# The first stage of a gated encoder layer in one written-out order: values in products of 512 columns, with masks and zero rows loaded in the block stage

## The chip, the core and the metric

The kernel runs on one core of a Trainium2 chip, in one launch. A time is the device time of that launch in microseconds (us); below it is told as the median of several runs. The trace is of one profiled execution.

A core has five engines that run their own instruction streams in order and wait for one another by semaphores: PE (TensorE, matmuls; PEld are its weight loads), DVE (VectorE), ACT (ScalarE), POOL (GpSimd) and SP (SyncE, which here only issues DMAs; its queue is SPq in the trace).

## What is computed

One encoder layer over 1024 tokens of width 1024, all in float32. Cut to what matters here:

```python
h = rmsnorm(x, attn_norm_g)
proj = h @ w_in
(c_q, c_kv, k_rope, z_mla, q_dil, k_dil, v_dil, z_dil, g_mla, g_dil) = jnp.split(proj, ...)
a_out = mla_attention(c_q, c_kv, k_rope, ...)         # 8 heads, latent ranks 256 and 128
d_out = dilated_mixture(q_dil, k_dil, v_dil, ...)     # 3 groups x 8 heads x 64
y_mla = (a_out * silu(z_mla)) @ w_o_mla
y_dil = (d_out * silu(z_dil)) @ w_o_dil
merged = sigmoid(g_mla + b) * y_mla + sigmoid(g_dil + b) * y_dil
out = rmsnorm(x + merged @ w_out, final_norm_g)
```

The change touches the projection: the latents `c_q`, `c_kv`, `k_rope` (416 columns of `w_in`) with the small products behind them, and the dilated values `v_dil` (three groups g of 512 columns each).

## The kernel before

Each float32 operand of a large product is split into a high and a low part, and a product is three matmuls: high by high, high by low, low by high (`mm3`, lines 145 to 147). A split is a copy on ACT (line 151) and a subtraction on POOL or DVE (line 152). The input, transposed and scaled by its norm gain, lies in `hTh` and `hTl` (in the trace `at_r`; in instruction lists `at_8192_r`) from the first microseconds on, in eight chunks `kc` of 128 rows.

The run has three parts. The **first stage** makes the latents, queries, keys and values of the latent attention, the dilated values, and the sums that the block stage needs. The **block stage** (`blocks`) makes dilated queries and keys and some gates in 16 items of seven parts each, a part being 4 x 3 matmuls of 512 columns into banks `st_a` to `st_d`. Then come the attention and the output. The block stage and what follows are issued in a written order (`manual_schedule`). The first stage is issued by the tile scheduler, which chooses the order of the instructions from `run` (lines 1598 to 1637).

In the first stage:

- `latent_proj` makes the 416 latent columns for eight groups t of 128 tokens: 8 x 8 `mm3` calls. ACT squares the results for the norm (lines 262 and 263), DVE copies them to `lat`.
- `token_factors` loads `x` in eight pieces `x_in`, sums their squares on ACT (line 276) and makes the per-token factor `rcol` by a chain of small DVE instructions (`rsqrt`, lines 204 to 210; line 278).
- `tables` makes the sine and cosine tables, stores them to DRAM (`s_cs`) and loads them back in copies `cs_m` and `cs_d`.
- `latents` scales `lat` by the factors (line 358), transposes it on PE (line 365), splits the transposes (lines 368 and 369), and makes queries, keys and values from them. Its 30 results are stored by way of two staging buffers `mla_st`.
- `dil_v(g, quad)` makes the dilated values: for each of three groups and two quads, for each of eight token groups, eight `mm3` calls into 256 columns of a bank `pj`. The result is scaled by `rcol` (lines 446 and 447, or 457) into `dv_st` or `dv_s` and stored.
- `block_sums` loads the input again in 16 pieces `y`, scales them on ACT (line 474), combines four at a time on POOL (lines 476 to 479), and splits the results on ACT and DVE into `s_h` and `s_l`.

PSUM has eight banks. In the first stage six serve the pool of `dil_v` and `latent_proj`, two the pool of `latents` (`NB_A = 6`).

Of the kernel before, what the change touches and what calls it, by code (L numbers as in the profile page):

```python
# [10 lines left out]
F32 = mybir.dt.float32  # L11
# [8 lines left out]
S = 1024  # L20
# [19 lines left out]
NB_A = 6  # L40
# [21 lines left out]
class Net:  # L62
# [170 lines left out]
    def latent_proj(self, lp, wl, xp, pj):  # L233
# [9 lines left out]
        for half in range(2):  # L243
            ps = [pj.tile([128, 512], F32, name="pj") for _ in range(4)]
            todo = []
            for kc in range(8):
                self.load_x(half, kc, xp)
                if half == 0:
                    raw = wl.tile([128, 416], F32, name="wl_raw", bufs=3)
                    self.dma(raw, a["wl"][kc])  # L250
                    self.split(raw, h[:, kc], l[:, kc], nc.gpsimd if kc % 2 else v)
                for t in range(4):
                    todo.append((kc, t))
            if half:
                todo.sort(key=lambda x: x[1])
            for kc, t in todo:
                ts = slice(512 * half + 128 * t, 512 * half + 128 * t + 128)
                self.mm3(ps[t][:, :416], self.hTh[:, kc, ts], self.hTl[:, kc, ts], h[:, kc], l[:, kc], kc == 0, kc == 7)
            for t in range(4):
                i = 4 * half + t  # L260
                junk = xp.tile([128, 256], F32, name="x_junk", bufs=2)
                nc.scalar.activation(out=junk, in_=ps[t][:, 0:256], func=AF.Square, accum_out=self.lss[:, 0, i:i + 1])
                nc.scalar.activation(out=junk[:, 0:128], in_=ps[t][:, 256:384], func=AF.Square, accum_out=self.lss[:, 1, i:i + 1])
                v.tensor_copy(self.lat[:, i, 0:400], ps[t][:, 0:400])
                v.tensor_copy(self.lat[:, i, 416:432], ps[t][:, 400:416])
            if half == 0:
                v.tensor_scalar(out=self.hb, in0=self.hb, scalar1=0.5, scalar2=None, op0=ALU.mult)

    def token_factors(self, xp, pp):

        nc, a = self.nc, self.a
        ss = xp.tile([128, 8], F32, name="x_ss", bufs=1)
        for t in range(8):
            x = xp.tile([128, D], F32, name="x_in")
            self.dma(x, a["x"][128 * t:128 * t + 128, :])
            nc.scalar.activation(out=x, in_=x, func=AF.Square, accum_out=ss[:, t:t + 1])
        y = self.rsqrt(ss, 1.0 / D, xp, 8)
        nc.vector.tensor_copy(self.rcol, y)
        pt = pp.tile([128, 512], F32, name="pj")
        nc.tensor.transpose(pt[:8, :128], y, self.ident)  # L280
        row = xp.tile([8, 128], F32, name="x_row", bufs=1)
        nc.vector.tensor_copy(row, pt[:8, :128])
        self.dma(self.rs, row)
        flat = self.rs.rearrange("a b -> (a b)")
        self.dma(self.R, flat.partition_broadcast(128))

    def tables(self, tp):
# [4 lines left out]
        self.dma(pi, a["positions"].partition_broadcast(64))  # L292
        ang = tp.tile([64, S], F32, name="ang", bufs=1)
# [21 lines left out]
    def rope(self, pa, pb, cos, sin, tp):  # L315
# [3 lines left out]
        m = [tp.tile([128, 512], F32, name=f"rope_m{i}") for i in range(4)]  # L319
# [6 lines left out]
    def up_weights(self, lp):  # L326
# [5 lines left out]
        for i in range(3):  # L332
            raw = lp.tile([128, 1024], F32, name="u_raw")
            n = 768 if i < 2 else 1024
            self.dma(raw[:, :n], a["wuq"][:, 768 * i:768 * i + 768] if i < 2 else a["wukv"])
            self.split(raw[:, :n], uh[:, i] if i < 2 else kh, ul[:, i] if i < 2 else kl, nc.gpsimd)
        return uh, ul, kh, kl

    def latents(self, up, lp, tp, pj):

        nc, a = self.nc, self.a
        v = nc.vector
        uh, ul, kh, kl = up
        for half in range(2):
            c512 = slice(half * 512, half * 512 + 512)

            r = self.rcol[:, 4 * half:4 * half + 4]
            sc = tp.tile([128, 2, 4], F32, name="lat_sc")
            for i in range(2):
                v.scalar_tensor_tensor(out=sc[:, i], in0=self.lss[:, i, 4 * half:4 * half + 4], scalar=(0.5, 1.0)[i], in1=r, op0=ALU.mult, op1=ALU.mult)  # L350
                v.tensor_tensor(out=sc[:, i], in0=sc[:, i], in1=r, op=ALU.mult)
            y = self.rsqrt(sc.rearrange("p a b -> p (a b)"), 1.0 / 128, tp, 8)
            for i in range(2):
                v.tensor_tensor(out=y[:, 4 * i:4 * i + 4], in0=y[:, 4 * i:4 * i + 4], in1=r, op=ALU.mult)
            for t in range(4):
# [294 lines left out]
    def blocks(self, items, tp, pp):  # L650
# [6 lines left out]
        for n in range(2):  # L657
            self.block_loads(n, items[n])
# [1082 lines left out]
```

## Time and profile before

| | |
|---|---|
| median of 3 runs | 1227.03 us (1226.45 to 1229.11) |
| the profiled execution's own time | 1229.1 us |
| its span, first to last instruction | 1227.1 us |
| PE busy | 1204.8 us, 98% of the span |
| DVE, ACT, POOL busy | 59%, 50%, 47% of the span |
| first matmul of the block stage | at 224.80 us |

The span is 2.0 us shorter than the execution's own time, and this execution is the slowest of the three runs: 2.1 us over their median. Times in the trace are counted from the span's start. A matmul's duration in the trace reaches beyond the start of the next one, since they are pipelined; what a matmul costs in a row of matmuls is the distance between starts.

### The profile page before, as it was taken

To read this page: it belongs to the slowest core of one execution; us is meant where nothing else is said; L and a number is where in the kernel's file an instruction comes from. 1 tells how busy PE (TensorE), PEld (TensorE's weight loads), DVE (VectorE), ACT (ScalarE), POOL (GpSimd) and SP (SyncE) were. 2 spreads that over 40 slices of the span, in tenths; PEclk is the share of its full clock that TensorE was granted. 3 is DMA by queue.
4 is the path that set the end of the run, shared out by engine and by line. 5 is a ranking of instruction groups with operands and counts; after the bars stand their busy time and mean duration, and the time that the engine had idled before them with its cause. 6 is when DMAs were issued, how large, how long until landed. Compare 5 with 4: busy or idle time off the path is not lost.

```text
span 1227.1 us, 19477 instructions
## 1 busy us (share of the span) xinstructions
PE 1204.8 (98%) x6909; PEld 1061.2 (86%) x6909; DVE 729.4 (59%) x1304; ACT 611.9 (50%) x1284; POOL 579.1 (47%) x490
## 2 busy tenths in 40 slices
PE   8989999999999999999999999999999999999997
PEld 7989999888888888888989898888888888888886
DVE  7483534376566753346666666647667767769442
ACT  6533335443434434446564756546556555654222
POOL 1361218777777777643365633416730101158322
PEclk9989999999999999999999999999999999999999
DMA  9858579356536544286889897965473445235241
GB/s 336 233 160 306 192 288 335 104 146 165 158 106 182 152 132 129 103 239 216 242 231 285 222 296 214 277 181 124 155 194 95 119 104 140 78 112 177 81 154 52
DMA packets 126416, 221.37 MB, mean 180 GB/s; under 512 B 28072, under 2 KB 60400, under 8 KB 121392
## 3 DMA queue, kind: packets, MB, share of 16 engines
q1 hardware_dynamic: 126320, 220.14, 60.4%
q8 instruction: 54, 0.88, 0.3%
q14 instruction: 42, 0.34, 0.1%
HBM read 149.24 MB, written 70.85 MB: 179 GB/s over the span
## 4 chain that ended last, share of the span: by engine, by line
PE 78%; DMA 9%; DVE 3%; ACT 3%; POOL 3%; issue 2%; SPq 1%; ACTq 0%; POOLq 0%; DVEq 0%
PE bank L145 6%; PE bank L147 6%; PE bank L146 6%; PE bank L871 4%; PE st_a L145 2%; PE st_a L147 2%; PE st_a L146 2%; PE st_c L146 2%; PE st_d L146 2%; PE st_d L145 2%; PE st_c L145 2%; PE st_d L147 2%; PE st_c L147 2%; PE bank L896 2%; PE bank L895 2%
## 5 line engine op out<-in xcount | busy, mean ns | idle before, releaser
L152 POOL TENSOR_TENSOR w_l<-w_raw,w_h 128x512 fp32r<-128x512 f32 x188 | 245.8, 1321 | 234.6 <-ACT w_h L151 183.2
L151 ACT CAST w_h<-w_raw 128x512 fp32r<-128x512 f32 x188 | 112.2, 620 | 106.3 <-POOL w_raw L496 90.6
L145 PE MATMUL bank<-at_r,w_h 128*128 128x512 f32 x344 | 141.3, 411 | 0.0
L146 PE MATMUL bank<-at_r,w_h 128*128 128x512 f32 x344 | 134.8, 392 | 0.6 <-POOL at_r L152 0.6
L147 PE MATMUL bank<-at_r,w_l 128*128 128x512 f32 x344 | 135.0, 392 | 0.0
L879 DVE TENSOR_TENSOR at_r<-bank,at_r 128x512 fp32r<-128x512 f32 x128 | 87.8, 687 | 68.0 <-ACT at_r L873 67.5
L873 ACT CAST at_r<-bank 128x512 fp32r<-128x512 f32 x128 | 74.9, 585 | 82.0 <-PE bank L871 81.2
L147 PE MATMUL pj<-w_h,at_r 128*128 128x256 f32 x384 | 109.7, 286 | 0.0
L146 PE MATMUL pj<-w_l,at_r 128*128 128x256 f32 x384 | 109.6, 286 | 0.0
L145 PE MATMUL pj<-w_h,at_r 128*128 128x256 f32 x384 | 109.6, 285 | 0.0
L496 POOL TENSOR_TENSOR w_raw<-w_raw 128x512 f32<-128x512 f32 x64 | 82.9, 1295 | 0.1
L871 PE MATMUL bank<-consts,at_f 128*128 128x128 f32 x512 | 76.8, 272 | 0.5 <-DVE at_r L879 0.5
L147 PEld LDWEIGHTS bank<-at_r,w_l 128*128 128x128 f32 x344 | 64.5, 188 | 14.5
L147 PEld LDWEIGHTS pj<-w_h,at_r 128*128 128x128 f32 x384 | 74.3, 194 | 1.0
L146 PEld LDWEIGHTS pj<-w_l,at_r 128*128 128x128 f32 x384 | 74.3, 193 | 0.8
L145 PEld LDWEIGHTS pj<-w_h,at_r 128*128 128x128 f32 x384 | 74.3, 193 | 0.7
L1144 DVE TENSOR_TENSOR at_r<-bank,at_r 128x512 fp32r<-128x512 f32 x64 | 43.9, 685 | 51.5 <-ACT at_r L1140 51.2
L146 PEld LDWEIGHTS bank<-at_r,w_h 128*128 128x128 f32 x344 | 65.0, 189 | 9.7 <-POOL at_r L152 1.0
L145 PEld LDWEIGHTS bank<-at_r,w_h 128*128 128x128 f32 x344 | 64.9, 189 | 8.8
L896 PE MATMUL bank<-at_r,at_r 128*128 128x256 f32 x256 | 66.9, 283 | 1.4 <-DVE at_r L879 1.4
L895 PE MATMUL bank<-at_r,at_r 128*128 128x256 f32 x256 | 66.9, 282 | 0.0
L1125 ACT ACTIVATE at_f<-at_f,at_f 128x256 f32<-128x256 f32 x128 | 64.1, 504 | 3.8 <-DVE at_f L1118 3.7
(325 smaller groups left out, 3328.2 us busy)
## 6 DMA issues: line engine op xcount, KB each, us to landing
w_raw<-wt SPq DMA_DIRECT2D x48, 512.0 KB, 3.7
at_r<-s_dq SPq DMA_DIRECT2D x32, 512.0 KB, 8.1
s_dk<-dq_st SPq DMA_DIRECT2D x80, 128.0 KB, 2.3
s_dv<-dv_st SPq DMA_DIRECT2D x32, 256.0 KB, 3.4
s_dq<-dq_st SPq DMA_DIRECT2D x64, 128.0 KB, 2.4
zt<-s_gt SPq DMA_DIRECT2D x32, 256.0 KB, 3.5
w_raw<-wv SPq DMA_DIRECT2D x12, 512.0 KB, 5.7
at_r<-s_dk SPq DMA_DIRECT2D x8, 576.0 KB, 10.3
```

What stands on the lines that cost most here:

```text
L145: mm(out, lh, rh, start=start, stop=False, skip_group_check=skip)
L146: mm(out, lh, rl, start=False, stop=False, skip_group_check=skip)
L147: return mm(out, ll, rh, start=False, stop=stop, skip_group_check=skip)
L151: self.nc.scalar.copy(out=h, in_=raw)
L152: sub.tensor_tensor(out=l, in0=raw, in1=h.bitcast(F32), op=ALU.subtract)
L496: self.nc.gpsimd.tensor_tensor(out=b[out], in0=b[x], in1=b[y], op=ALU.subtract)
L871: self.nc.tensor.transpose(pt[:, o:o + 128], self.P[k, b][:, 128 * kc:128 * kc + 128], self.ident)
L873: self.nc.scalar.copy(out=h, in_=pt)
L879: self.nc.vector.tensor_tensor(out=l, in0=pt, in1=h.bitcast(F32), op=ALU.subtract)
L895: mm(out, vv[:, kc], ph[:, x], start=kc == 0, stop=False)
L896: mm(out, vv[:, kc], pl[:, x], start=False, stop=kc == 7)
L1125: nc.scalar.activation(out=p, in_=p, func=AF.Exp, scale=-1.0, bias=nm, accum_out=den)
```

## The change

The scheduler no longer orders the first stage. `manual_schedule` now covers the whole run, and a new function `first_stage` writes the order out.

- **Values of 512 columns.** `dil_v` gives way to `v_load`, `v_split` and `v_part`. The two quads of a group lie side by side in one weight tile of 512 columns. The work is cut into 48 parts c: 16 for each group g, each for one token group t and one half s of the chunks kc, 4 `mm3` calls of 512 columns. Two parts fill a bank, and the second of them scales and stores it. Four banks serve the values, four the latents.
- **Latents between the parts.** `latents` becomes a generator of 36 steps. From part 6 on, 1.75 steps follow each part. The up weights are split on DVE instead of POOL, and `mla_st` has five buffers, which the raw up weights use first.
- **First products.** The latent products are ordered by hand (`first_products`); the loads of `x` and the tables are placed between them.
- **Block sums in steps.** `block_sums` becomes a generator; one step follows each part from part 30 on, with `y` in three buffers.
- **Block operands.** The first item's weights are loaded at part 35, and its first five operands are split in parts 44 to 47, with the subtraction on DVE. `w_h` and `w_l` of the blocks alternate between the two pools in fours instead of singly.
- **Moved into the block stage.** Masks, zero rows of `s_dk` and `s_dv`, the zero fill of `s_dq2` and the products of `cs_d` with the token factors (`self.R`) now stand at parts 2 to 24 of the block stage.

The core of the diff:

```diff
-NB_A = 6
+LATENTS_BEGIN, LATENTS_PACE = 6, 1.75
...
+    def v_split(self, s, i, eng):
+
+        wp = (self.wp, self.wpx)[s]
+        h = wp.tile([128, 512], F32R, name="w_h", bufs=4)
+        l = wp.tile([128, 512], F32R, name="w_l", bufs=4)
+        self.split(self.v_raw[s][i // 2][:, i % 2].rearrange("p q c -> p (q c)"), h, l, eng)
+        self.v_w[s, i] = h, l
+
+    def v_part(self, c, pool, tp):
+
+        g, r = divmod(c, 16)
+        part, t = divmod(r, 4)
+        t += 4 * (part // 2)
+        s = (0, 1, 1, 0)[part] ^ (g & 1)
+        begin = part % 2 == 0
+        if begin:
+            self.v_ps[t] = pool.tile([128, 512], F32, name="pj")
+        ps = self.v_ps[t]
+        sl = slice(128 * t, 128 * t + 128)
+        for i in range(4):
+            kc = 4 * s + i
+            self.mm3(ps, self.hTh[:, kc, sl], self.hTl[:, kc, sl], *self.v_w[s, i], begin and i == 0, not begin and i == 3)
+        if begin:
+            return
...
     def block_sums(self, sp, tp):
...
+        for kc in range(3):
+            loads(kc)
+        yield
+        yield
+        scaled(0)
+        yield
+        for kc in range(4):
+            added(kc)
+            if kc:
+                parts(kc - 1)
+                if kc == 1:
+                    loads(3)
+                yield
+            yield
+            if kc < 3:
+                scaled(kc + 1)
+                yield
+        yield
+        parts(3)
...
+            for c in range(48):
+                self.v_part(c, pj, vp)
+                g, r = divmod(c, 16)
+                if 2 <= c < 10:
+                    self.latent_scaled(c - 2)
+                if 5 <= c < 8:
+                    next(weights)
+                if c == 20:
+                    self.token_row(tp, pl)
+                first, second = (0, 1) if g & 1 else (1, 0)
+                if r == 6:
+                    self.v_load(g + 1, first)
+                if r == 14:
+                    self.v_load(g + 1, second)
+                if g < 2 and 12 <= r < 15:
+                    for i in ((0, 1), (2,), (3,))[r - 12]:
+                        self.v_split(first, i, nc.gpsimd if g == 0 else nc.vector)
+                if g and r < 3:
+                    for i in ((0, 1), (2,), (3,))[r]:
+                        self.v_split(1 - (g & 1), i, nc.gpsimd if g == 1 else nc.vector)
+                if c == 29:
+                    self.cos_d, self.sin_d = self.table(dpool, "cs_d", 0)
+                if c == 35:
+                    self.block_loads(0, self.block_items[0], (self.wp, None))
+                if c >= LATENTS_BEGIN and latents:
+                    steps += LATENTS_PACE
+                    while steps >= 1 and latents:
...
+                elif later and c >= 30:
+                    next(later, None)
+                if c >= 44:
+                    for j in ((0, 1), (2,), (3,), (4,))[c - 44]:
+                        self.block_minus(j, self.block_items)
+                        self.block_operand(j, self.block_items, nc.vector)
...
+            if x in (2, 3, 4, 5):
+                y, c = (self.cos_d, self.sin_d)[x // 2 - 1], slice(512 * (x % 2), 512 * (x % 2) + 512)
+                self.nc.gpsimd.tensor_tensor(out=y[:, c], in0=y[:, c], in1=self.R[:, c], op=ALU.mult)
...
+            if x in (4, 8, 12, 16):
+                i = x // 4 - 1
+                self.dma(self.dq[2][i].rearrange("e c r h (a b) f m -> (e c r) (h a) (b f m)", a=2), self.zero.unsqueeze(1).to_broadcast([128, 4, 512]))
...
+            ctx.enter_context(tc.manual_schedule())
```

How the instructions move is read from the order in which each engine gets them. On PE, where the first transposes of the latents stand among the value products, before (`w_h`, `w_l`: value weights; `lat`: the latents; `pj`: a bank):

```order
L145 MATMUL pj<-w_h,at_8192_r 128x256
L365 MATMUL pj<-consts,lat 128x128 x2
L146 MATMUL pj<-w_l,at_8192_r 128x256
L147 MATMUL pj<-w_h,at_8192_r 128x256
L145 MATMUL pj<-w_h,at_8192_r 128x256
L365 MATMUL pj<-consts,lat 128x128 x2
```

The same place now, at the end of part 6 (the transposes are line 421 of the changed file):

```order
L145 MATMUL pj<-w_h,at_8192_r 128x512
L146 MATMUL pj<-w_l,at_8192_r 128x512
L147 MATMUL pj<-w_h,at_8192_r 128x512
L421 MATMUL pj<-consts,lat 128x128 x4
L145 MATMUL pj<-w_h,at_8192_r 128x512
```

The value matmuls are twice as wide, and the transposes of a step stand together after a whole part. From the first matmul of the block stage on, PE's list is the same as before.

On SP, where the pieces `y` of the block sums are loaded, before (`s_mv`, `s_dv_69`: results to DRAM; `wt`: weights of the first block item):

```order
L141 DMA s_mv<-mla_st 128x1024
L141 DMA s_dv_69<-dv_st 32x4x512
L141 DMA w_raw<-wt 128x1024
L141 DMA y_1534<-xt 128x512
L141 DMA y_1537<-xt 128x512
```

The same loads now, from part 28 on (`wv`: value weights of group 2):

```order
L141 DMA s_dv_69<-dv_st 32x4x1024 x2
L141 DMA cs_d<-s_cs 32x2048 x4
L141 DMA s_dv_69<-dv_st 32x4x1024
L141 DMA w_raw<-wv 128x2x256 x4
L141 DMA y_1570<-xt 128x512
L141 DMA y_1572<-xt 128x512
```

The four loads of `cs_d`, which stood far ahead of the `y` loads, now stand just before the last value weights and these. Each DMA uses one of eight semaphores in turn, and its issue waits until the DMA that used that one before it has landed, so that the first `y` load waits for the first `cs_d` load.

On ACT, from the last scaled bank of group 1 (part 31) on, now (line 552: the scaling of `y`; line 151: the high part of a split):

```order
L522 ACTIVATE dv_st<-pj,rcol 128x8x64
L151 CAST w_h<-w_raw 128x512 x2
L552 ACTIVATE y_1570<-y_1570,consts 128x512
L552 ACTIVATE y_1572<-y_1572,consts 128x512
L552 ACTIVATE y_1574<-y_1574,consts 128x512
L552 ACTIVATE y_1576<-y_1576,consts 128x512
L151 CAST w_h<-w_raw 128x512 x2
```

Before, the first four scalings stood between scaled banks of the values, with no value weight behind them:

```order
L474 ACTIVATE y_1540<-y_1540,consts 128x512
L474 ACTIVATE y_1543<-y_1543,consts 128x512
L457 ACTIVATE dv_s_2236<-pj,rcol 128x256
L474 ACTIVATE y_1558<-y_1558,consts 128x512
L474 ACTIVATE y_1561<-y_1561,consts 128x512
L151 CAST s_h<-y_1543 128x512
```

Now the last two of the four value weights that parts 36 to 39 need are copied behind the scaling of four `y` pieces.

More of the change, by code (lines that the diff above doesn't have):

```diff
@@ new lines, in first_products @@
+        for kc in range(8):
+            self.load_x(0, kc, xp)
+            raw = wl.tile([128, 416], F32, name="wl_raw", bufs=3)
+            self.dma(raw, a["wl"][kc])
+            self.split(raw, h[:, kc], l[:, kc], nc.gpsimd if kc % 2 else v)
+            for t in range(4):
+                product(t, kc)
+            if kc == 5:
+                next(tables)
+        for kc in range(8):
+            self.load_x(1, kc, xp)
+        for t in range(4, 8):
+            for kc in range(8):
+                product(t, kc)
@@ new lines, in first_products, with load, squares @@
+        ss = xp.tile([128, 8], F32, name="x_ss", bufs=1)
+        xs = {}
+        def load(t):
+            xs[t] = xp.tile([128, D], F32, name="x_in")
+            self.dma(xs[t], a["x"][128 * t:128 * t + 128, :])
+        def squares(t):
+            nc.scalar.activation(out=xs[t], in_=xs[t], func=AF.Square, accum_out=ss[:, t:t + 1])
+        self.v_load(0, 0)
+        for t in range(3):
+            load(t)
+        next(tables)
+        for t in range(4):
+            squared(t)
+            taken(t)
@@ new lines, in first_products @@
+        for i in range(4):
+            self.v_split(0, i, nc.gpsimd)
+        for t in range(3):
+            squares(t)
+            if t < 2:
+                load(t + 3)
+        next(tables)
+        squared(4)
+        taken(4)
+        self.v_load(0, 1)
+        for t in range(5, 8):
+            squares(t - 2)
+            load(t)
+            if t == 5:
+                next(tables)
+            if t == 6:
+                for i in range(4):
+                    self.v_split(1, i, nc.gpsimd)
+            squared(t)
+            taken(t)
@@ L277, in token_factors, with token_row @@
+        for t in range(6, 8):
+            squares(t)
+        run_all(tables)
         y = self.rsqrt(ss, 1.0 / D, xp, 8)
-        nc.vector.tensor_copy(self.rcol, y)
+        v.tensor_copy(self.rcol, y)
+        v.tensor_scalar(out=self.hb, in0=self.hb, scalar1=0.5, scalar2=None, op0=ALU.mult)
+    def token_row(self, tp, pp):
+        nc = self.nc
         pt = pp.tile([128, 512], F32, name="pj")
-        nc.tensor.transpose(pt[:8, :128], y, self.ident)
-        row = xp.tile([8, 128], F32, name="x_row", bufs=1)
+        nc.tensor.transpose(pt[:8, :128], self.rcol, self.ident)
+        row = tp.tile([8, 128], F32, name="mla_st", bufs=5)
@@ L345, in latents @@
             c512 = slice(half * 512, half * 512 + 512)
[L347 to L355, printed above, removed]
[L356 to L358 removed]
+            cos, sin = self.cos_m[:, c512], self.sin_m[:, c512]
             nh = lp.tile([128, 3, 512], F32R, name="lat_h", bufs=1)
@@ L483, in block_loads, with scaled @@
-    def block_loads(self, n, item):
-        raw = [self.raw_pools[n % 2].tile([128, 8, 128], F32, name="w_raw", bufs=2) for _ in range(2)]
+                    x = y[kc, i, k] = tp.tile([128, 512], F32, name=f"y{i}{k}", bufs=3)
+                    self.dma(x, a["xt"][i, :, kc + 4 * k])
+        def scaled(kc):
+            for i in range(2):
+                for k in range(2):
+                    c = kc + 4 * k
+                    nc.scalar.mul(y[kc, i, k], y[kc, i, k], self.ga[:, c:c + 1])
@@ L486, in block_loads @@
+    def block_loads(self, n, item, pools):
+        raw = [pools[n % 2].tile([128, 8, 128], F32, name="w_raw", bufs=2) for _ in range(2)]
         for i in range(2):
@@ L650, in blocks @@
     def blocks(self, items, tp, pp):
[L652 to L654 removed]
+        pools = self.wp, tp
         places = 7 * len(items)
         steps, ps = {}, {}
[L657 to L660 removed]
@@ L1637, in run @@
+                self.block_items = [(T_QK + (g * 2 + quad) * 4 + which * 2, g, quad, which) for quad in range(2) for g in range(3) for which in range(2)] + [(T_ZM + i,) for i in BLOCK_GATES]
+                cp.tile([128, 896], F32, name="masks")
+                self.masks = self.hand(2048, 896)
+                self.first_stage(cp, dpool, sums)
                 self.rings()
```

357 lines of the change are left out of this document (175 added, 182 removed).

## Prediction

> **What bounds the kernel now.** First the page's head and the waits of PE over the first stage.
>
> ```profile
> PE 1204.8 (98%) x6909; PEld 1061.2 (86%) x6909; DVE 729.4 (59%) x1304; ACT 611.9 (50%) x1284; POOL 579.1 (47%) x490
> ```
>
> ```profile
> PE pj L145 <- ACT wl_h L151: 5.8, 1, 5.8
> PE pj L365 <- DVE lat_l L369: 3.4, 1, 3.4
> PE st_a L145 <- ACT dv_s L457: 2.0, 1, 2.0
> PE pj L365 <- DVE lat L358: 1.2, 1, 1.2
> PE pj L145 <- DVE mla_st L152: 0.4, 1, 0.4
> ```
>
> PE works nearly all the time, so a change pays in two ways: less time for PE's own work, or fewer waits. These five waits are 12.8 us, of which 5.8 come before the first matmul. The others fall mostly at the first latent transposes (1.2 and 3.4) and at the first block matmul (2.0), which waits for ACT to empty a value bank. The timeline of PE has the end of the stage:
>
> ```profile
> 224.80 0.50 PE L145 MATMUL st_a<-at_r,w_h 128*128 128x512 f32 x1 [2.02 <-ACT dv_s L457]
> ```
>
> From here on PE's list is the same in both kernels, so I forecast by how much this moment comes earlier. Next, the stretches behind the two longest waits (length; busy time of PE, PEld, DVE, ACT, POOL; granted clock; DMA):
>
> ```profile
> 74.00:78.00 4.00, 4.00 (x19) 3.87 (x20) 2.52 (x5) 0.24 (x1) 3.85 (x4) 0.50 0.92 276
> 78.00:82.00 4.00, 4.00 (x30) 4.00 (x29) 3.21 (x5) 2.53 (x5) 3.33 (x2) 0.82 0.57 189
> 226.00:228.00 2.00, 2.00 (x7) 1.58 (x6) 0.00 (x0) 0.15 (x1) 2.00 (x2) 0.55 0.28 82
> 228.00:230.00 2.00, 2.00 (x7) 1.55 (x7) 0.00 (x0) 0.81 (x2) 0.37 (x1) 0.60 0.79 260
> ```
>
> A wait costs more than itself. Behind the 3.4 us one the clock was 0.50 and then 0.82: 4 x 0.50 + 4 x 0.18 = 2.7 us of PE's time lost. Behind the 2.0 us one it was 0.55 and 0.60: 2 x 0.45 + 2 x 0.40 = 1.7 us.
>
> **The change part by part.** *Values of 512 columns.* Starts of matmuls in PE's timeline, in the last value product, in the block stage, and in a latent product between narrower ones, and one of three like groups:
>
> ```profile
> 220.22 0.28 PE L146 MATMUL pj<-w_l,at_r 128*128 128x256 f32 x1
> ...
> 222.50 0.28 PE L147 MATMUL pj<-w_h,at_r 128*128 128x256 f32 x1
> ```
>
> ```profile
> 300.00 0.39 PE L145 MATMUL st_d<-at_r,w_h 128*128 128x512 f32 x1
> ...
> 305.67 0.39 PE L146 MATMUL st_b<-at_r,w_h 128*128 128x512 f32 x1
> ```
>
> ```profile
> 163.51 0.40 PE L145 MATMUL pj<-lat_h,ukv_h 128*128 128x512 f32 x1
> 163.74 0.40 PE L146 MATMUL pj<-lat_l,ukv_h 128*128 128x512 f32 x1
> ```
>
> ```profile
> L145 PE MATMUL pj<-w_h,at_r 128*128 128x256 f32 x384 | 109.6, 285 | 0.0
> ```
>
> The first pair is 19 steps apart: 2.28 / 19 = 0.120 us for 256 columns. The second is 25 apart: 5.67 / 25 = 0.2268 us for 512. Before, 3 x 384 = 1152 matmuls take 138.2 us; now 576 take 130.6 us: **7.6 us saved**. At the 0.23 of the third pair it would be 132.5 us and 5.7 saved. I take the first, since a part has twelve wide matmuls in a row, as in the block stage.
>
> [...]
>
> *The old waits.* The 1.2, 3.4 and 2.0 us go if nothing takes their place: 6.6 us, and 2.7 + 1.7 = 4.4 us of clock with them. At the block start, the latents' four banks are long empty, and the scaled value banks belong to the second block item. That makes 7.6 + 6.6 + 4.4 = **18.6 us** at most. What is late next?
>
> *First transposes.* They now stand behind part 6 and need four tokens' groups scaled by DVE.
>
> ```profile
> 10.09 1.42 PE L145 MATMUL pj<-wl_h,at_r 128*128 128x416 f32 x4
> 11.35 0.35 PE L146 MATMUL pj<-wl_l,at_r 128*128 128x416 f32 x1
> ...
> 13.62 0.35 PE L146 MATMUL pj<-wl_l,at_r 128*128 128x416 f32 x1
> ```
>
> ```profile
> 52.62 0.17 DVE L210 SCALAR_TENSOR_TENSOR rs_y<-rs_u,rs_y 128x8 f32<-128x8 f32 x1
> 52.81 0.17 DVE L278 COPY rcol<-rs_y 128x8 f32<-128x8 f32 x1
> ```
>
> ```profile
> L358 DVE TENSOR_SCALAR lat<-lat,rs_y 128x128 f32<-128x128 f32 x8 | 6.7, 832 | 0.0
> L358 DVE TENSOR_SCALAR lat<-lat,rs_y 128x256 f32<-128x256 f32 x8 | 2.8, 346 | 0.0
> L152 DVE TENSOR_TENSOR mla_st<-pj,mla_st 128x512 fp32r<-128x512 f32 x16 | 11.1, 692 | 23.1 <-ACT mla_st L151 23.1
> L151 ACT CAST mla_st<-pj 128x512 fp32r<-128x512 f32 x16 | 9.4, 586 | 22.5 <-DMA s_kn<-mla_st 9.1 <-PE pj L147 5.4 <-DMA s_qn<-mla_st 3.4
> ```
>
> PE: sixteen latent matmuls have started before 11.35 (a chunk is twelve, and four more stand in the first row), and twelve start from 11.35 to 13.62, so 0.189 us each; 176 more end at 44.6. Seven parts of 12 x 0.2268 = 2.72 us bring PE to 63.7. DVE: `rcol` at 53.0 as before, 18 small instructions 0.19 apart (3.4), four groups at 0.35 + 0.83 + at most 0.35 (6.1), and two banks emptied in between at 0.69: 63.9. So the two arrive together. I take 0.5 us of wait. The bounds are 0, and 3.5 with 2.7 of clock if `rcol` comes 3 us later, since the last loads of `x` now stand behind squares that ACT takes in order.
>
> *Weights behind `y`.* This is the new wait that I trust least. The last value weights (needed from part 36 on) are copied by ACT behind four scalings of `y`, and the first `y` load is issued only when the first `cs_d` load, issued behind part 29, has landed (SP's list).
>
> ```profile
> w_raw<-wv SPq DMA_DIRECT2D x12, 512.0 KB, 5.7
> ...
> y<-xt SPq DMA_DIRECT2D x16, 256.0 KB, 5.5
> ...
> cs_d<-s_cs SPq DMA_DIRECT2D x4, 256.0 KB, 10.1
> ```
>
> ```profile
> L151 ACT CAST w_h<-w_raw 128x512 fp32r<-128x512 f32 x30 | 17.7, 621 | 6.2 <-POOL w_raw L496 3.7 <-DMA w_raw<-wv 1.7 <-PE pj L147 0.7
> ...
> L474 ACT ACTIVATE y<-y,consts 128x512 f32<-128x512 f32 x16 | 11.1, 718 | 2.0 <-DMA y<-xt 1.9
> ```
>
> ```profile
> L152 DVE TENSOR_TENSOR s_l<-y,s_h 128x512 fp32r<-128x512 f32 x16 | 19.2, 1230 | 29.0 <-ACT s_h L151 28.5
> ```
>
> From the `cs_d` issue: 10.1 to land, 5.5 for `y`, 4 x 0.72 = 2.9 to scale, 0.6 to copy the third weight, 1.2 on DVE: 20.3 us. PE gets there after six and a half parts less the 0.59 + 0.69 that part 29's bank takes before the issue: 17.7 - 1.3 = 16.4. That is a wait of 3.9 us. If `cs_d` lands in the 5.5 us of `y`, which is as large, it is 15.7 us and no wait. Before, `cs_d` had many other loads in flight, now fewer, so I take the middle, 2.0 us, and 1.0 for the clock (a wait of 2.0 cost 1.7 once, one of 1.2 nothing in the rows). [...]
>
> *The rest* I put at 1.0 us, a little over twice the small wait of 0.4 in the first list. The order gives ACT, DVE and SP the same number of latent results as before, with five staging buffers where there were two.
>
> *Block stage.* Four products of `cs_d` move to POOL's parts 2 to 5, and 13 DMAs to SP's parts 4 to 24.
>
> ```profile
> 224.80:523.30 298.50, 298.50 (x1310) 246.99 (x1311) 165.89 (x265) 124.31 (x236) 216.13 (x171) 0.99 0.49 139
> ```
>
> ```profile
> L1632 POOL TENSOR_TENSOR cs_d<-cs_d,at_f 128x512 f32<-128x512 f32 x4 | 6.2, 1569 | 19.3 <-DMA s_dv<-dv_st 19.3
> ```
>
> POOL is busy 72% there. In four parts, 10.9 us, it has 7.9 + 6.2 = 14.1 us to do and falls 3.2 us behind, while operands are split five parts (13.6 us) ahead. DMA is at 0.49. I cost this at nothing; without that lead it would be 3.2 us.
>
> *Sum.* 18.6 - 0.5 - 2.0 - 1.0 - 1.0 = 14.1 us. The profiled execution would go from 1229.1 to 1215.0; against the median of 1227.0 that is **1213 us** (1212.9).
>
> **The rivals.**
>
> *The first transposes still wait* (chance 0.09). If `rcol` comes 3 us later, DVE is late by 3.5 us and the clock costs 2.7: 18.6 - 3.5 - 2.7 - 4.0 = 8.4, thus 1218.6 us. For it: the two arrive within 0.2 us of each other by the sum. Against it: the order puts nothing else on DVE there.
>
> *Width pays only by columns* (0.04). If a wide matmul costs two narrow ones, 0.240, the first term is gone and the time is 1212.9 + 7.6 = 1220.5. For it: the 0.23 in a mixed stretch. Against it: 25 steps at 0.2268 with the same operands in their other roles. [...]
>
> *ACT and POOL take turns* (0.09), and the kernel is slower. In parts 30 to 47 ACT empties value banks in its order behind copies that wait for POOL's sums.
>
> ```profile
> L476 POOL TENSOR_TENSOR y<-y,y 128x512 f32<-128x512 f32 x4 | 5.2, 1298 | 6.0 <-ACT y L474 6.0
> L477 POOL TENSOR_TENSOR y<-y,y 128x512 f32<-128x512 f32 x4 | 5.9, 1487 | 0.2
> L478 POOL TENSOR_TENSOR y<-y,y 128x512 f32<-128x512 f32 x4 | 6.2, 1560 | 0.3
> L479 POOL TENSOR_TENSOR y<-y,y 128x512 f32<-128x512 f32 x4 | 6.3, 1563 | 1.6 <-ACT y L474 1.4
> L151 ACT CAST s_h<-y 128x512 fp32r<-128x512 f32 x16 | 9.8, 617 | 8.7 <-POOL y L476 2.7 <-POOL y L478 2.6 <-POOL y L479 1.9
> ```
>
> A round is 2.9 of scaling, 5.9 of sums and 2.5 of copies. Strung on one another they make 11.3 us, against three parts of 2.72 = 8.2: 3.1 us late in each of four rounds, 12.4 in all, with 3.9 at part 36 and the clock at 1.7 for each of four waits: 23.1 us, thus 1227.0 - 18.6 + 23.1 = 1231.5 us. Against it: the scaling of the next round stands ahead of the copies, so that POOL can go on meanwhile, and 5.9 fits in 8.2. It decides when `y` lands so late that POOL finds nothing scaled.
>
> *The change moves no time* (0.03): the stage would be held by loads, not PE. Against it stand 98% and PE's unbroken rows.
>
> **How the numbers follow.** My forecast has 0.75. Its bounds are all new waits gone (18.6, thus 1208.4) and the wider pitch with 3.9 + 1.7 at part 36 and the rest (16.7 - 7.1 = 9.6, thus 1217.4). The range of 1206 to 1222 us takes these, 2 us below for waits that also vanish elsewhere, and the first two rivals: 0.88 of the cases, some 0.8 with what the durations leave open. About 0.2% (2.5 us) is what a measurement of this kernel can tell from no change. Faster by more: 0.75 + 0.09 + 0.04 = 0.88; within it 0.03; slower 0.09.
>
> **What would show it.** In the profile of the changed kernel: the first block matmul at about 212 us instead of 224.80 (the 14.1 less the 1.7 of clock that fall behind it); 576 value matmuls 0.227 us apart; no wait of 3.4 us at the transposes; a wait of about 2 us on DVE's `w_l` at part 36; the clock at 1.0 behind the block start; and no new wait from there on. The forecast is wrong if the first block matmul comes before 207 or after 218 us, or if PE waits in the block stage.

## The result, and the profile after

| | before | after |
|---|---|---|
| median of the first comparison, 6 runs each | 1228.36 us (1226.45 to 1229.26) | 1219.16 us (1216.37 to 1222.17) |
| after over before | | 0.9924, 95% interval 0.9907 to 0.9941 |
| the profiled execution's own time | 1229.1 us | 1216.4 us |
| its span | 1227.1 us | 1214.6 us |
| first matmul of the block stage | 224.80 us | 208.49 us |

One execution of the experiments, in `moved_back`, took 1488.66 us at a granted clock of 0.753 and is left out of the times there. The changed kernel is faster: 9.2 us by the medians, 12.5 by the two spans. The spans flatter it, since the profiled execution is the fastest of six after and the second slowest of six before. In a second comparison (the experiment `again`) it took 1216.85 against 1229.51 us, 12.7 us less, ratio 0.99 (0.9878 to 0.9921). The forecast was 14.1 less.

The page's first line, and all waits of PE in the run:

```profile
PE 1193.9 (98%) x6333; PEld 1027.4 (85%) x6333; DVE 740.5 (61%) x1286; ACT 606.7 (50%) x1260; POOL 558.3 (46%) x474
```

```profile
PE pj L145 <- ACT wl_h L151: 6.1, 1, 6.1
PE bank L1069 <- DVE at_r L1052: 4.1, 3, 2.5
PE pj L146 <- DVE w_l L152: 1.6, 2, 0.9
PE bank L1305 <- ACT at_f L1298: 0.9, 3, 0.6
PE bank L146 <- POOL at_r L152: 0.5, 1, 0.5
PE bank L1044 <- DVE at_r L1052: 0.5, 1, 0.5
PE right L1281 <- DMA at_r<-s_dk: 0.2, 1, 0.2
```

All waits of the old first stage are gone but the one ahead of the first matmul. One new one stands there, at part 36. In PE's timeline, with the first transposes and one product of the block stage's last item:

```profile
63.43 0.60 PE L421 MATMUL pj<-consts,lat 128*128 128x128 f32 x4
...
176.28 0.50 PE L146 MATMUL pj<-w_l,at_r 128*128 128x512 f32 x1 [0.90 <-DVE w_l L152]
...
177.98 0.50 PE L146 MATMUL pj<-w_l,at_r 128*128 128x512 f32 x1 [0.74 <-DVE w_l L152]
...
184.01 0.39 PE L145 MATMUL pj<-w_h,at_r 128*128 128x512 f32 x1
...
208.26 0.39 PE L147 MATMUL pj<-w_h,at_r 128*128 128x512 f32 x1
208.49 0.39 PE L145 MATMUL st_a<-at_r,w_h 128*128 128x512 f32 x1
...
496.13 0.39 PE L145 MATMUL st_a<-at_r,w_h 128*128 128x512 f32 x1
```

The same product before:

```profile
514.20 0.39 PE L145 MATMUL st_a<-at_r,w_h 128*128 128x512 f32 x1
```

From 184.01 to 208.26 are 107 steps, 0.2266 us each. The transposes wait for nothing. The block stage starts 224.80 - 208.49 = 16.3 us earlier, and its last item 514.20 - 496.13 = 18.1 earlier, since no clock is lost at its start. In between PE never waits (stretches as in the prediction):

```profile
224.00:512.00 288.00, 288.00 (x1273) 238.46 (x1272) 165.98 (x266) 119.21 (x227) 209.57 (x173) 1.00 0.52 149
```

So far 18.1 us are won, but the span is only 12.5 shorter: **5.6 us are lost again** in the attention, where the two kernels have the same instructions. PE's waits there (line 1069: values of the latent attention), and what DVE waits for just ahead of them:

```profile
847.10 0.38 PE L1069 MATMUL bank<-at_r,at_r 128*128 128x256 f32 x1 [1.41 <-DVE at_r L1052]
...
889.27 0.39 PE L1069 MATMUL bank<-at_r,at_r 128*128 128x256 f32 x1 [2.45 <-DVE at_r L1052]
```

```profile
845.76 0.69 DVE L1617 TENSOR_TENSOR at_f<-at_f,at_f 128x512 f32<-128x512 f32 x1 [4.60 <-DMA at_f<-s_rr]
...
887.92 0.69 DVE L984 SCALAR_TENSOR_TENSOR at_f<-zt,bank 128x512 f32<-128x512 f32 x1 [5.60 <-DMA zt<-s_gt]
```

The same DVE instructions before (with a wait of PE of 1.17 us behind the second and none behind the first):

```profile
861.32 0.69 DVE L1444 TENSOR_TENSOR at_f<-at_f,at_f 128x512 f32<-128x512 f32 x1 [3.21 <-DMA at_f<-s_rr]
...
902.23 0.69 DVE L811 SCALAR_TENSOR_TENSOR at_f<-zt,bank 128x512 f32<-128x512 f32 x1 [4.34 <-DMA zt<-s_gt]
```

DVE names DMA as what it waited for; PE's row names only DVE, which stands between. Both loads (shares of the softmax, `s_rr`, and the first gate, `s_gt`) come 1.3 to 1.4 us later than before, measured by DVE's wait. Behind the longer wait the clock falls as well:

```profile
890.00:892.00 2.00, 2.00 (x9) 1.61 (x7) 2.00 (x3) 1.62 (x3) 0.00 (x0) 0.56 0.82 218
892.00:894.00 2.00, 2.00 (x12) 1.80 (x10) 0.77 (x2) 1.77 (x4) 0.10 (x1) 0.58 0.71 277
```

That is 2 x 0.44 + 2 x 0.42 = 1.7 us. Together 1.41 + (2.45 - 1.17) + 1.7 = 4.4 of the 5.6; the rest lies in small waits: the lead over the kernel before falls from 18.2 us at 526 us of the changed kernel's trace to 17.1 at 763.

### The profile page after: what moved, and what is told of

Its sections match the earlier page's. It is cut to its first block, busy times and chain, and to the rows that moved or that the text cites. A ratio compares the mean times of both kernels' runs of the same rounds, so it can differ in the third digit from the quotient of the medians.

```text
span 1214.6 us, 18187 instructions
## 1 busy us (share of the span) xinstructions
PE 1193.9 (98%) x6333; PEld 1027.4 (85%) x6333; DVE 740.5 (61%) x1286; ACT 606.7 (50%) x1260; POOL 558.3 (46%) x474
## 4 chain that ended last, share of the span: by engine, by line
PE 82%; DMA 10%; POOL 2%; DVE 2%; ACT 1%; issue 1%; SPq 1%; POOLq 0%; ACTq 0%; DVEq 0%
PE bank L146 6%; PE bank L147 6%; PE bank L145 5%; PE pj L146 5%; PE pj L147 5%; PE pj L145 5%; PE bank L1044 4%; PE st_d L145 2%; PE st_c L145 2%; PE st_a L145 2%; PE st_a L146 2%; PE st_c L146 2%; PE st_d L146 2%; PE st_d L147 2%; PE st_c L147 2%; PE st_a L147 2%
## 5 line engine op out<-in xcount | busy, mean ns | idle before, releaser
L152 POOL TENSOR_TENSOR w_l<-w_raw,w_h 128x512 fp32r<-128x512 f32 x175 | 230.2, 1328 | 214.8 <-ACT w_h L151 163.9
L1046 ACT CAST at_r<-bank 128x512 fp32r<-128x512 f32 x128 | 74.9, 585 | 84.9 <-PE bank L1044 84.3
L146 PE MATMUL pj<-w_l,at_r 128*128 128x512 f32 x192 | 75.0, 391 | 1.6 <-DVE w_l L152 1.6
L145 PE MATMUL pj<-w_h,at_r 128*128 128x512 f32 x192 | 75.3, 392 | 0.0
L147 PE MATMUL pj<-w_h,at_r 128*128 128x512 f32 x192 | 74.8, 390 | 0.0
L1313 ACT CAST at_r<-bank 128x512 fp32r<-128x512 f32 x64 | 37.5, 586 | 53.3 <-PE bank L1305 52.2
L1044 PEld LDWEIGHTS bank<-consts,at_f 128*128 128x128 f32 x512 | 59.3, 140 | 1.3 <-DVE at_r L1052 0.9
L1069 PEld LDWEIGHTS bank<-at_r,at_r 128*128 128x128 f32 x256 | 48.7, 190 | 10.1 <-DVE at_r L1052 4.9
```

The costliest lines, as they stand in the source:

```text
L145: mm(out, lh, rh, start=start, stop=False, skip_group_check=skip)
L146: mm(out, lh, rl, start=False, stop=False, skip_group_check=skip)
L147: return mm(out, ll, rh, start=False, stop=stop, skip_group_check=skip)
L152: sub.tensor_tensor(out=l, in0=raw, in1=h.bitcast(F32), op=ALU.subtract)
L1044: self.nc.tensor.transpose(pt[:, o:o + 128], self.P[k, b][:, 128 * kc:128 * kc + 128], self.ident)
L1046: self.nc.scalar.copy(out=h, in_=pt)
```

## The experiments

Each is compared with the kernel before on the same chip. Medians are of 5 to 12 runs. The first four ran together; with them the changed kernel itself stands at 0.99 (`again`; 0.9924 in the first comparison). `pool_sum`, `gates_first`, `all_three` and `before_again` ran on another chip, where the changed kernel was not measured; they are set against 0.99 by their ratio to the kernel before. A ratio's interval reaches about 0.002 (2 to 3 us) to either side, so smaller differences between two edits are not told apart by the times.

**again.** No edit.

> The changed kernel once more, unaltered. In its first profile the first block matmul starts 16.3 us earlier than before (208.49 against 224.80), the last item of the block stage 18.1 us earlier, but the span is only 12.5 us shorter: 5.6 us are given back in the attention, 1.41 us at 847.1 and 2.45 us (with 1.7 of clock behind it) at 889.3, where DVE waits for a load of s_rr and for one of s_gt. Theory A (the loss belongs to the new timing): both waits come again, 1 to 3 us each, and the time is 9 to 13 us under the kernel before. Theory B (the loss is the chance of one execution, since the instructions and their order are the same in both kernels there): one wait or both are gone or of another length, by over 1 us, while the first block matmul stays within 1 us of 208.5.

The first block matmul came at 209.19 us. PE waited 2.09 us at 847.50 and 2.42 at 889.65. Theory A: the loss belongs to the kernel. (Part 36 cost 0.61 + 0.89 + 0.73 here.)

**narrow.**

```diff
-            self.mm3(ps, ..., *self.v_w[s, i], ...)
+            for q in range(2):
+                x = slice(256 * q, 256 * q + 256)
+                self.mm3(ps[:, x], ..., *(y[:, x] for y in self.v_w[s, i]), ...)
```

> Every value matmul of 512 columns is issued as two of 256, in the same order and with the same operands. By the starts in the trace before (0.120 us for 256 columns, 0.2268 for 512) 1152 x 0.120 - 576 x 0.2268 = 7.6 us are lost: first block matmul at about 216.1 instead of 208.5, time 7.6 us above the changed kernel's. Rival 1 (a matmul costs its columns only): no loss, 208.5. [...]

Its first block matmul:

```profile
215.53 0.40 PE L145 MATMUL st_a<-at_r,w_h 128*128 128x512 f32 x1
```

That is 7.0 us later than in the changed kernel, and 7.4 with the waits at part 36 taken off both (1.3 here, 1.6 there). The time was 1223.56 us, 6.7 above `again` (ratio 0.9955, 0.9938 to 0.9971). The rival falls; the width pays what the starts said.

**cs_early.**

```diff
-                if c == 29:
+                if c == 24:
                     self.cos_d, self.sin_d = self.table(dpool, "cs_d", 0)
```

> The four loads of cs_d are issued behind part 24 instead of part 29. Theory (they are what holds the last value weights and the y loads behind them up): PE's waits of 0.90 and 0.74 us at part 36 go, the first block matmul comes at about 206.9, 1.6 us earlier, and the time is 1.6 us under the changed kernel's. Rival (the weights' own load, or ACT's order with the scaling of y ahead of them, sets the wait): the waits stay within 0.5 us.

```profile
177.54 0.50 PE L146 MATMUL pj<-w_l,at_r 128*128 128x512 f32 x1 [0.73 <-DVE w_l L152]
...
208.05 0.39 PE L145 MATMUL st_a<-at_r,w_h 128*128 128x512 f32 x1
```

One of the two waits went, the other stayed on the same split by DVE: by the two profiles `cs_d` is the cause of 0.9 of the 1.6 us. The block stage comes 0.4 us earlier than in the changed kernel's first profile and 1.1 earlier than in `again`, not at the expected 206.9. 1215.71 us, 1.1 under `again`, with overlapping intervals (0.9868 to 0.9903): the times alone don't show a gain.

**moved_back.** The bodies go, unaltered, from `blocks` to `first_stage` (the conditions alone are shown):

```diff
-            if x in (2, 3, 4, 5):
-            if x == 20:
-            if x in (22, 24):
-            if x in (4, 8, 12, 16):
+                if 42 <= c < 46:
+                if c == 8:
+                if c in (37, 39):
+                if c in (38, 40, 42, 44):
```

> The pieces that the change moved into the block stage stand in the first stage again: the masks' loads behind part 8, zero rows and the zero fill of s_dq2 behind parts 37 to 44, the products of cs_d on POOL behind parts 42 to 45. Theory (the move hid nothing that PE waited for): the time is within 1.5 us of the changed kernel's, with no wait over 0.5 us at the block start. Rival (the move is part of the gain): POOL's 6.2 us and the fills delay the block sums or the first block operands, PE waits 2 to 6 us between parts 40 and 48 or at the first block matmuls, and the clock falls behind it.

1217.71 us (five executions), ratio 0.991 (0.9888 to 0.9932): 0.9 above `again`, within the theory. Only the times speak: whether PE waited at the block start was not read from a trace.

**half.** As `narrow`, but only in three banks of group 0 (the rest of the loop works with `n`):

```diff
-            for q in range(2):
-                x = slice(256 * q, 256 * q + 256)
+            n = 2 if g == 0 and t < 3 else 1
+            for q in range(n):
+                x = slice(512 // n * q, 512 // n * (q + 1))
```

This and the next ask why the two loads come later in one kernel than in the other. The trace has packets of queue 8, labelled instruction, of 16 KB each; I call them code loads. In the stretch from the issue of the `s_rr` loads to DVE's product the DMA view has, for the changed kernel (packets, MB, the times of the packets as a share of 16 engines' span; KB, median us to landing):

```profile
q1 hardware_dynamic: 1715, 2.29, 94.6%
q8 instruction: 1, 0.02, 0.9%
...
at_f<-s_rr SPq DMA_DIRECT2D x2, 128.0 KB, 7.8
```

and for the kernel before:

```profile
q1 hardware_dynamic: 1630, 2.03, 103.1%
...
at_f<-s_rr SPq DMA_DIRECT2D x2, 128.0 KB, 6.3
```

One code load more, and 1.5 us more to land. (0.9% of 16 engines over 8.4 us is 1.2 us of one engine.) Over the whole run, page of before and of the changed kernel:

```profile
q8 instruction: 54, 0.88, 0.3%
```

```profile
q8 instruction: 50, 0.82, 0.3%
```

PE has 2 x 6909 = 13818 matmuls and weight loads before and 12666 after: 256 and 253 to a packet. The change takes 1152 away, 4.5 x 256, so that by this count each code load falls half a distance away from where it fell. `half` (12810) has 50 such packets, `whole` (12954) has 51. `narrow` has the count of before again, 13818, and 54 packets; in it the waits of line 1069 (line 1071 there) were 1.3 us in all. DVE, ACT and POOL have 1286, 1260 and 474 instructions in it as in the changed kernel, so the packets go with PE's list; that they carry PE's code is argued from these counts.

> 72 of the 576 wide value matmuls (group 0, token groups 0 to 2) are issued as two of 256 columns, so PE's list holds 144 more instructions (a matmul and its weight load each) before the block stage. Theory (PE's code is loaded in blocks of 16 KB, one every 20 us or so in the attention; a block that falls into the loads of s_rr and s_gt keeps one of the 16 DMA engines busy for about a microsecond and makes them land later; 144 instructions shift the blocks by about half their distance): the first block matmul comes 0.95 us later than in the changed kernel, but no block falls into these two loads, PE's waits in the attention fall from 4.1 and 4.7 us to about 1.3 as in the kernel of narrow matmuls, and the time is 2 to 4 us under the changed kernel's. Rival (those waits come from the attention's being earlier, or from the change's other loads): the waits stay at 4 to 5 us, and the time is 1 us above.

**whole.** The same with `t < 6`.

> As the run before, but 144 wide matmuls are issued as two (token groups 0 to 5 of group 0): 288 more instructions, a little over one whole distance of the code loads. Theory: the blocks fall into the two loads again, the waits in the attention are 3.5 to 5 us as in the changed kernel, and the time is 1.9 us above the changed kernel's, so 4 to 5 us above the run with half as many. Rival (more instructions, or a later start of the attention, mend the waits): the waits are 1.3 us as in the run with half as many.

Waits of line 1069 (1072 here): `half` 1.9 us in all, none at `s_rr`; `whole` 2.8, of which 1.08 at `s_rr` and 1.52 at the gate. In `whole` the code load fell into the 2.4 us ahead of the issue of the `s_rr` loads, not behind it, so my shift missed its place and its expected 3.5 to 5 us did not come. The first block matmul came at 208.65 us in `half`, where 209.4 was expected, and at 211.33 in `whole`. The duration from issue to DVE's product, in ten profiles (`moved_back` is left out, `both_waits` has the product later, `pool_sum` and `all_three` have it on POOL), with whether the DMA view of that stretch holds a code load:

| profile | issue, product starts | us | code load |
|---|---|---|---|
| narrow | 848.40, 854.90 | 6.5 | none |
| before | 854.29, 861.32 | 7.0 | none |
| before_again | 852.59, 859.75 | 7.2 | none |
| half | 843.18, 850.39 | 7.2 | none |
| whole | 839.92, 848.02 | 8.1 | just ahead |
| after | 837.33, 845.76 | 8.4 | one |
| cs_early | 838.04, 846.88 | 8.8 | one |
| gates_first | 843.03, 852.02 | 9.0 | one |
| again | 837.04, 846.15 | 9.1 | one |
| sched | 846.47, 855.63 | 9.2 | one |

The two groups don't overlap. The two loads landed, by their median, 7.8 to 8.5 us behind the issue in the five with a code load and 7.4 in `whole`, against 5.8 to 6.5 in the four without one. So code load and late landing go together; that the one makes the other is argued from this, not shown. The time didn't follow: `half` 1216.44 us (0.9904, 0.9885 to 0.9923) and `whole` 1217.41 (0.9906, 0.9891 to 0.9922), where 4 to 5 us between them were expected. The profile of `half` has a possible reason:

```profile
530.54 0.35 PE L1284 MATMUL right<-at_r,at_r 128*128 128x256 f32 x1 [1.52 <-DMA at_r<-s_dk]
...
768.67 2.00 PE L1395 MATMUL right<-at_f,at_f 128*128 128x64 f32 x16 [1.66 <-DMA at_f<-s_dk]
```

These two waits are not in the changed kernel, and in `half` a code load stands in the 5.7 us ahead of each. So it does in the 4 us ahead of a wait of 2.12 us for `s_dk` in `narrow`, at 538.06. A code load that leaves one transfer meets another; that these waits come from it is argued, not shown. Behind the wait at 768.67 the clock fell as well: from 771.01 to 773.57 products of 512 columns start 0.43 us apart instead of 0.23. But this execution of `half`, 1220.92 us, is the slowest of its six, so the others need not have these waits. Its granted clock is 0.95 elsewhere, where the changed kernel has 1.00, though its block matmuls start 0.2267 us apart as there.

**both_waits.**

```diff
-LAST_STEPS = {..., 11: 19, 12: 20}
+LAST_STEPS = {..., 11: 20, 12: 21}
...
-            if u == 3 and h < 6:
+            if u == 3 and h < 6 and k != 8:
                 self.mla_load_v(h + 2)
...
-            if u == 3 and h < 6:
+            if u == 3 and h < 6 and k != 7:
                 self.mla_load_qk(h + 2)
...
                 self.mla_gated(k)
+                if k == 8:
+                    self.mla_load_qk(3)
+                    self.mla_load_v(3)
```

> The two waits of the attention get more slack, with the first stage unaltered: the last weighted sum of the fourth pair is taken one tick (2.4 us) later, and the query, key and value loads of head 3 are issued behind the first gate loads instead of ahead of them. Theory (PE waits there only because DVE stands behind loads that land late): the waits of 1.41 to 2.09 us at 847 and of 2.4 us at 889 go, with the clock lost behind the second, and the time is 4 to 5.5 us under the changed kernel's. Rival (DVE is late there for its own work, or the next load takes their place): under 1.5 us gained.

```profile
854.75 1.11 PE L1044 MATMUL bank<-consts,at_f 128*128 128x128 f32 x4 [4.89 <-DVE at_r L1052]
```

1220.8 us, 3.9 above `again` (ratio 0.993, 0.9912 to 0.9948). My edit was at fault: one tick later, the factor's buffer already has a gate piece loaded into it (`s_zs`), so the product uses that, not the factor, and DVE waits for it. The wait at the gate was gone (line 1069: 0.2 us). So the two were parted, the first in another way.

**pool_sum.**

```diff
         def step11():
-            weighted(2, 1, v)
+            weighted(2, 1, p if pair == 3 else v)
```

> The changed kernel, where for the last pair the second half of group 2's weighted sum is multiplied on POOL instead of DVE, so that POOL and not DVE stands behind the load of s_rr. Theory (PE waits at 847 us only because DVE's at_r stands behind that product): the wait of 1.41 us (2.09 in the second profile) goes and the time is about 1.5 us under the changed kernel's. Rival (POOL's own wait makes its next results late, and PE waits for POOL instead): a wait of 1 us or more elsewhere before 870 us, and no gain.

```profile
891.60 0.39 PE L1069 MATMUL bank<-at_r,at_r 128*128 128x256 f32 x1 [3.31 <-DVE at_r L1052]
```

The wait at `s_rr` is gone, and the one at the gate is 0.9 us longer than in the changed kernel: 1219.15 us, ratio 0.9911 (0.9888 to 0.9934), no gain. PE comes to the second load earlier and waits there.

**gates_first.** The lower three pieces of the diff of `both_waits` alone.

> The changed kernel, where the query, key and value loads of head 3 (2 MB) are issued behind the first gate loads instead of ahead of them. Theory (the first gate lands late because it queues behind these loads, and a code load among them makes it later): the wait of 2.4 us at 889 goes, with the 1.7 us of clock behind it, the time is 2.4 to 4.1 us under the changed kernel's, and the wait at 847 stays between 1.0 and 2.1. Rival (the next gate, or head 3 itself, is late instead): a new wait of over 1 us behind 890.

The wait at the gate is gone, none of over 1 us came behind 890, and that at `s_rr` was 1.96 us; 1215.77 us, ratio 0.9877 (0.9851 to 0.9902), 0.0023 or 2.8 us under `again`. That is near the theory's lower end, but the two intervals overlap, so that the wait's going is shown and the gain in time is not. In this profile part 36, with 0.61 + 0.90 + 0.73 us of waits, cost clock as well, and the first block matmul came at 212.30:

```profile
178.00:180.00 2.00, 1.27 (x4) 0.87 (x4) 1.56 (x2) 1.28 (x3) 1.92 (x2) 0.55 1.04 414
180.00:182.00 2.00, 2.00 (x6) 1.61 (x5) 1.86 (x2) 1.40 (x3) 1.92 (x3) 0.50 1.02 414
182.00:184.00 2.00, 2.00 (x6) 1.52 (x5) 2.00 (x3) 0.94 (x2) 1.92 (x2) 0.50 0.45 152
184.00:186.00 2.00, 2.00 (x8) 1.55 (x8) 1.62 (x1) 0.74 (x2) 1.92 (x2) 0.74 0.18 68
```

**all_three.** The diffs of `pool_sum`, `gates_first` and `cs_early` in one.

> The two edits of the attention together, and the loads of cs_d behind part 24. Theory (three separate waits): PE's waits in the attention fall under 1 us in all, that at part 36 to 0.7, and the time is the sum of the three gains under the changed kernel's, 5 to 6 us, at about 1211. Rival (DMA has the same bytes to move, so that another load is late by as much): not over 2.5 us under the changed kernel's.

```profile
PE bank L1069 <- DVE at_r L1052: 0.8, 2, 0.6
PE bank L1308 <- ACT at_f L1301: 0.7, 3, 0.4
PE pj L146 <- DVE w_l L152: 0.6, 1, 0.6
```

**1211.28 us** (1209.38 to 1215.09), ratio 0.9848 (0.9824 to 0.9872), faster than either kernel. Against 0.99 that is 0.0052 or 6.4 us, by the medians more than the gains one by one (1.1, none, 2.8): neither wait is left for the other to pass to. The intervals of `all_three` and `again` don't overlap, so this gain is shown; how it divides among the three edits is not. PE's waits in the attention add up to 3.1 us, not to under 1 as expected, against 6.2 in the changed kernel. The granted clock was 1.00 in the stretches of the two waits (836 to 848 and 880 to 892 us), where it cost the changed kernel 1.7 us, and 0.999 in the mean of the run against 0.997.

**sched.**

```diff
-            ctx.enter_context(tc.manual_schedule())
...
-                    self.blocks(self.block_items, tp, pp)
+                    with tc.manual_schedule():
+                        self.blocks(self.block_items, tp, pp)
```

> The changed kernel with its first stage left to the tile scheduler, from the block stage on in the written order: the same wide matmuls and the same pieces, in an order that the scheduler chooses. Theory (7 us of the gain are the width, the other 9 at the block start come from the written order): PE waits 4 to 10 us at the transposes, at weights or at the block start, and the first block matmul comes at 213 to 219 us. Rival (the width and the buffers are all that counts, and any order will do): within 1.5 us of 208.5.

```profile
29.26 0.72 PE L147 MATMUL pj<-wl_h,at_r 128*128 128x416 f32 x1 [2.32 <-DVE at_r L231]
...
213.04 0.39 PE L145 MATMUL st_a<-at_r,w_h 128*128 128x512 f32 x1
```

```profile
28.00:32.00 4.00, 2.74 (x7) 2.17 (x8) 4.00 (x4) 0.00 (x0) 2.14 (x2) 0.62 1.04 384
32.00:36.00 4.00, 4.00 (x14) 3.86 (x13) 3.50 (x5) 1.73 (x2) 0.00 (x0) 0.53 0.13 47
```

The block stage starts at 213.04, 4.5 us later than in the written order, and the one large wait of its first stage lies in the first products: 2.32 us, and 4 x 0.38 + 4 x 0.47 = 3.4 of clock. 1223.31 us, ratio 0.9951 (0.9933 to 0.9969). Another wait of PE, 3.28 us for ACT at 533.93, stands early in the attention and takes part of the 6.5 us by which this run is slower than `again`. So in this profile the scheduler keeps 11.8 of the 16.3 us with the new pieces and buffers; the order as such is worth 4.5 at the block start. My theory's 9 was too much, and "any order will do" is wrong too.

**before_again.** The kernel before, unaltered.

> The kernel before once more, unaltered, for a second profile. Theory (its code loads miss the two loads of the attention in every execution, since they depend on the number of instructions alone): the wait at the first gate is 1.2 us again within 0.5, there is none at the load of s_rr, and the waits behind the block stage add up to 3 to 4 us. Rival (its first profile was lucky): one of the two waits is 2 us or more, or the waits add up to over 5 us. The time is that of the kernel before within its spread.

```profile
PE pj L145 <- DVE mla_st L394: 2.6, 1, 2.6
PE pj L365 <- DVE lat_l L369: 0.7, 1, 0.7
...
226.34 0.50 PE L145 MATMUL st_a<-at_r,w_h 128*128 128x512 f32 x1 [2.14 <-ACT dv_s L457]
...
902.43 0.39 PE L896 MATMUL bank<-at_r,at_r 128*128 128x256 f32 x1 [1.61 <-DVE at_r L879]
```

No wait at `s_rr`, 1.61 us at the gate, waits behind the block stage of 3.3 us in all: as expected. 1228.4 us. The first stage lost its time in another way than in the first profile: 9.1 us of waits behind the first matmul instead of 7.3, the longest at a product of the latents (2.6), with 0.7 instead of 3.4 at the transposes.

## Why the prediction was right or wrong

- **Faster, and mostly for the reasons given: right.** 1219.16 us lies in the range, 6 us above the forecast of 1213; a gain of 14.1 was forecast, and 9.2 and 12.7 were measured. That it came so near is in part luck: the new waits of the stage were put 2.9 us too high (4.5 us for the 1.6 of the first profile) and the loss in the attention at nothing.
- **Width, 7.6 us: right.** 7.0 to 7.4 by `narrow`; in the changed kernel the starts lie 0.2266 us apart at 512 columns in a row (184.01 to 208.26).
- **The old waits and their clock, 6.6 + 4.4: gone as said.** `sched` shows that the new pieces and buffers take away most of them, not the written order alone. The terms were sized by one execution: in `before_again` the three waits are 0.7, 0.7 and 2.1 us, with 5.6 us of others beside them. The clock's part is less firm than I had it: there the mean granted clock of 0.998 leaves about 2.5 us lost in the whole run, 1.7 of them from 96 to 104 us, so the 2.14 us at the block start can't have cost another 1.7, as 2.02 did in the first profile.
- **First transposes, 0.5: nothing was lost**; they came at 63.43, where I had PE at 63.7.
- **Part 36, 2.0 + 1.0: right in size, half right in cause.** 1.6 to 2.2 us of wait in the changed kernel's two profiles and in five more with the same part; the clock took 3.4 us there in `gates_first` and nothing in the first profile. `cs_d` explains one of two waits.
- **The rest, 1.0 in the stage, and nothing in the block stage:** no other wait came in the first profile, PE was busy 288.00 of 288.00 us, and `moved_back` moved the time by 0.9 us, less than can be told.
- **"No new wait from there on": wrong. This step failed.** In the profiled executions the stage gave 18.1 us where I had 14.1, and the attention took 5.6 back: 12.5. I had taken the attention as fixed since its instructions are the same, but its loads are not: DVE waited 1.3 to 1.4 us longer for two of them and PE behind it, 1.41 and 2.45 us; `pool_sum` and `gates_first` show that these waits hang on the two loads. Why the loads are late is argued: with 1152 fewer instructions on PE, a code load fell into each of the two stretches on which DVE waits. For `s_rr` the ten profiles agree with that. For the gate it is weaker: its DVE product starts 10.1 to 10.6 us behind the first issue in the changed kernel, `again`, `cs_early` and `pool_sum`, and 9.0 to 9.8 in the kernel before, `before_again`, `narrow` and `half`, but 9.8 and 9.4 in `sched` and `whole`, which have a code load there. And by the times of `half` moving the code loads doesn't win the time back.
- What stays open: why single executions of the changed kernel differ by 6 us. Part 36 is one piece of it: in five profiles with the same first stage (the changed kernel, `again`, `pool_sum`, `both_waits`, `gates_first`) the first block matmul came at 208.49, 209.19, 210.80, 211.24 and 212.30. Of that the clock took nothing at part 36 in the changed kernel and in `again` (steps of 0.23 us but for the first behind each wait, 0.34), 1.5 in `pool_sum` (seven steps from 178.81 to 181.97 in 3.16 us instead of 1.70) and 3.4 in `gates_first`, with 1.6 us of waits for DVE in each of them.

## What to carry to other kernels

When a change removes instructions far from a tuned stretch, the stretch behind can still lose, as here 5.6 us: look in the changed profile for the first engine that waits for a load, not only for the engine that PE names. Give such loads slack against bulk transfers (here 2 MB of head 3 ahead of a 256 KB gate; behind it, in `gates_first`, the wait of 2.45 us was gone), and mend neighbouring waits together, since one mended alone may only lengthen the next. Price a matmul by the distance of starts at its own width (here 0.120 us at 256 columns, 0.2266 at 512).

## What the runs showed of the hardware

- A code load of 16 KB on its own queue stood beside slow landings: two loads of 128 KB, issued together, landed 7.8 to 8.5 us behind the issue in the five profiles with a code load in their stretch (the changed kernel, `again`, `cs_early`, `gates_first`, `sched`), 7.4 in `whole`, with one just ahead, and 5.8 to 6.5 in the four without (`narrow`, the kernel before, `before_again`, `half`).
- In the first profiles of the two kernels the edges of the clock lie in one raster. While PE works, the granted clock falls to 0.50 at 72.61 and 226.21 us before and rises again at 79.43 and 229.62: 2 x 3.41 us, 43 x 3.413 and 3.41 between these edges. In the changed kernel it falls at 890.26 and rises at 893.67, 3.41 behind. Of the stretches of 3.41 us at full clock in this raster, from 12 us on, those in which PE stood idle for 2.03 and 2.01 us before, and for 2.42 in the changed kernel, were followed by one at half clock, which costs 1.7 us; those with 1.16 and 1.17 before, and with 1.22 in the changed kernel, were not. The 2.45 us at 889.27 in the changed kernel, 2.42 of them in one stretch:

```profile
886.84:890.26 3.42, 0.99 (x8) 0.99 (x9) 2.34 (x3) 0.00 (x0) 0.00 (x0) 1.00 0.53 163
890.26:893.67 3.41, 3.41 (x12) 2.82 (x11) 2.51 (x4) 3.24 (x6) 0.00 (x0) 0.50 0.83 266
```

  And 2.20 us in `cs_early`, ending at 890.17, cost nothing:

```profile
885.16:888.57 3.41, 2.81 (x17) 2.22 (x15) 0.00 (x0) 0.59 (x1) 0.00 (x0) 1.00 0.71 240
888.57:891.98 3.41, 1.81 (x11) 1.65 (x12) 3.15 (x5) 0.69 (x1) 0.00 (x0) 1.00 0.60 196
891.98:895.39 3.41, 3.41 (x23) 3.04 (x22) 1.84 (x3) 3.19 (x7) 0.59 (x1) 1.00 0.75 262
```

  So a wait's length alone doesn't tell what it costs here: 2.02 and 2.45 us cost 1.7 each, 2.20 nothing, and the 2.14 of `before_again` no 1.7 either. That the 2.20 us lie across an edge of the raster, as 0.60 and 1.60 us in these rows, is my estimate from the 3.41 us of the two kernels; with the clock at 1.00 throughout, the rows show no edge.
